# A block-product scheme for the up-projection of a channel mixer, with GpSimd forming the weight sums

## The chip, the cores and the metric

One NeuronCore of one Trainium2 chip runs the whole program. The metric is device time in microseconds of one execution; the time before is the median of three runs.

## What is computed

The program is one inference step of a one-layer decoder trunk on 520 tokens: 512 of a new prompt and 8 single-token samples. A token mixer (windowed attention beside a gated delta rule) is followed by a channel mixer, which is where the change lies. Cut to that part:

```python
x = x + rmsnorm(mix, ln_mix_post)
h = rmsnorm(x, ln_ffn_pre)                                   # 520 tokens x 2048
up, ffn_new = causal_dwconv(h @ w_ffn_in, ffn_buf, ffn_conv_w)  # 2048 -> 11264, then width 3 over tokens
gate, val = jnp.split(up + ffn_conv_b, 2, axis=-1)           # 5632 each
f = (jax.nn.gelu(gate, approximate=True) * val) @ w_ffn_out  # 5632 -> 2048
x = x + rmsnorm(f, ln_ffn_post)
```

All inputs and outputs are float32.

## The kernel before, in words

Features lie on the 128 partitions and tokens run along the free axis. Every large product is taken in three passes on TensorE: weights and operands are each split into a rounded part (`hi`) and a rest (`lo`), and hi x hi, hi x lo and lo x hi are added up in PSUM. ScalarE rounds (a cast, L127 for weights), VectorE subtracts (`lo`, L128). The tokens are kept as two parts, A of 256 and B of 264 columns, in pools `xsA` and `xsB`, 16 buffers each.

The stages follow each other in code order; a scheduler of the language places instructions on the engines, guided by priorities (`HI()` raises one) and explicit `issue_after` edges. Each engine then works through its own list in order. Weight loads are issued by SyncE (`Q`), and most small transfers of the mixer by GpSimd (`B`, `G`).

Stage 1 projects the inputs and runs the token mixer. Stage 2 is the output projection, once per token part; `mid2` then adds the residual, forms the FFN's operand `H2` and writes x1 to HBM. Stage 3 is the FFN. The 88 feature tiles of the up-projection are 44 gate tiles f and 44 value tiles 44 + f. `u_tile` makes one of them: 16 blocks of 128 rows by 3 passes by 2 token parts are 96 TensorE instructions (L160, in `gemm`). VectorE then multiplies by the norm's row (L1114) into `U`, and `pair` runs the width-3 convolution (ScalarE L1122, VectorE L1124 twice per tile), GeLU, the gating product (VectorE, L1134) and the split of the result into `act`. Two small GpSimd copies per tile (L1140, L1141) keep the last rows. After four f (a part p; there are 11), `ffn_out(p - 1)` runs the down-projection of the part before: 16 output tiles of 24 instructions, each added into `yacc` by VectorE (L1188). So up- and down-projection alternate. `part_end` handles the 8 samples of a part (L1159 to L1171).

The order of weights is the list `units`: `next_unit` keeps two units ahead of use, each loaded as two halves of 512 KB into `raw`, and each half split as two tiles of 128x512. The shifted caches are copied HBM to HBM in 128 pieces, three after each f (`shift(3)`).

Of the kernel before, what the change touches and what calls it, by code (L numbers as in the profile page):

```python
# [20 lines left out]
TAGS = ("bankS", "bankT", "bankP", "bankX")  # L21
NCV = 5
NA, NB = 256, 264
# [16 lines left out]
def trunk(ctx, tc, I, O):  # L40
# [51 lines left out]
    def ffn_units(p):  # L92
        u = []
        for f in range(4 * p, 4 * p + 4):
            u += [I["w_ffn_in"][f], I["w_ffn_in"][44 + f]]
        return u
    units += ffn_units(0) + ffn_units(0)
    for p in range(1, NP):
        units += ffn_units(p)
        units += [I["w_ffn_out"][p - 1, g].rearrange("p a b c -> p (a b) c") for g in range(4)]  # L100
    for _ in range(1):
        units += [I["w_ffn_out"][NP - 1, g].rearrange("p a b c -> p (a b) c") for g in range(4)]
# [5 lines left out]
    def emit_half(u, hf):  # L108
        with HI():
            raw = wraw.tile([128, 8, 128], F32, name="raw")  # L110
            lastw[0] = Q.dma_start(raw, units[u][:, hf * 8:hf * 8 + 8, :])
            if u >= len(units) - 4:
                # the last part is used twice: kept whole where the FFN's operand lay
                for q in range(4):
                    b = hf * 8 + q * 2
                    t = xsA.tile([128, 2, NA], F32R, name="xa") if q % 2 else xsB.tile([128, 2, NB], F32R, name="xb")
                    r = raw[:, q * 2:q * 2 + 2, :].rearrange("p a b -> p (a b)")
                    S.copy(t[:, 0, 0:256], r)  # L118
                    V.tensor_sub(t[:, 1, 0:256], r, t[:, 0, 0:256].bitcast(F32))
                    for j in range(2):  # L120
                        wt[u, "b", b + j] = (t[:, 0, j * 128:j * 128 + 128], t[:, 1, j * 128:j * 128 + 128])
                return
            for q in range(2):
                hi = whi.tile([128, 4, 128], F32R, name="hi")
                lo = wlo.tile([128, 4, 128], F32R, name="lo")
                r = raw[:, q * 4:q * 4 + 4, :]
                S.copy(hi, r)  # L127
                V.tensor_sub(lo, r, hi.bitcast(F32))  # L128
                wt[u, hf * 2 + q] = (hi, lo)
# [22 lines left out]
    def gemm(blks, X, ks, parts="AB"):  # L152
        ps = gps.tile([128, 1024], F32, name="ps")
        n = len(ks)
        for i, k in enumerate(ks):
            wh, wl = wblk(*blks[i])
            for j, (w, b) in enumerate(((wh, 0), (wh, 1), (wl, 0))):
                for part in parts:
                    o, w_ = SEG[part]
                    PE.matmul(ps[:, 256 + o:256 + o + w_], w, X[k][part][:, b, :],  # L160
# [3 lines left out]
    def split(dsts, src, o, w, scale=None):  # L164
        """dsts: fp32r tile [128,2,w]; src fp32 AP [128,w]."""
# [81 lines left out]
    def bias_tables():  # L247
        rb = Pd.tile([32, H], F32, name="rb")
        B.dma_start(rb, I["rel_bias"])
        for dst, o, n in ((FD, 0, 640), (FS, 640, 400)):  # L250
# [4 lines left out]
            for a in range(0, n, 512):  # L255
# [3 lines left out]
                if n == 640:  # L259
                    # the scores of the prompt are kept with the opposite sign  # L260
# [65 lines left out]
    # gates: rows 0..7 beta, rows 32..39 the decay  # L326
# [5 lines left out]
    def gates(ps):  # L332
# [29 lines left out]
    def gate_cols():  # L362
# [4 lines left out]
        # the samples' decay and beta on all partitions  # L367
# [30 lines left out]
    def col_sums(c, o, keep):  # L398
        """squared norms of q (o = 0) or k (o = 4), tokens of a chunk on partitions."""
# [147 lines left out]
    def scan(c):  # L547
# [48 lines left out]
        # state  # L596
# [12 lines left out]
        # outputs  # L609
# [32 lines left out]
    def over_partitions(rows):  # L642
        """sums over the partitions, on all of them."""
# [4 lines left out]
    def sample_dn():  # L648
# [16 lines left out]
        # partitions (sample, value head, half of dk)  # L665
# [80 lines left out]
    def rows_of(src, last):  # L746
        """[128 d, (h, b)] -> DRAM [b][h][d]: the queries, or the last row of a shifted cache."""
# [39 lines left out]
        # maximum over the rows of a sample  # L787
# [22 lines left out]
    def sample_values():  # L810
# [22 lines left out]
        # the new key and value  # L833
# [10 lines left out]
        # 16 rows carry the new key  # L844
# [82 lines left out]
    for idx, m in enumerate(mt_order):  # L927
# [11 lines left out]
        elif m < 8:  # L939
            with HI():  # L940
                V.scalar_tensor_tensor(attm[:, m, :], ps[:, 256:776], -SC, R1, op0=OP.mult, op1=OP.mult)
            V.tensor_copy(qs[:, m, :], attm[:, m, 512:520])
        elif m < 24:
            h = m % 8
            t = Ppa.tile([128, T], F32, name="kT" if m < 16 else "vT", bufs=2)
            with HI():
                V.tensor_mul(t, ps[:, 256:776], R1)
# [68 lines left out]
    R2 = rrow.tile([128, T], F32, name="R")  # L1016
    H2 = [{} for _ in range(KT)]

    def mid(part, also):
        """mix -> x1 = x + norm(mix) and the FFN's operand."""  # L1020
# [6 lines left out]
        for m in range(KT):  # L1027
# [18 lines left out]
    def mid2(part, acc, mxs, wk):  # L1046
        o, w = SEG[part]
        sl = xsA if part == "A" else xsB
        nm = "xa" if part == "A" else "xb"
# [4 lines left out]
        for g in range(8):  # L1054
            xr = wk.tile([128, 2, NB], F32, name="x2", bufs=2)
            x = xr[:, :, :w]
            Q.dma_start(x, I["xT"][:, 2 * g:2 * g + 2, o:o + w])
            y = mxs[g]
            V.tensor_mul(y, y, rp[:, None, :w].to_broadcast([128, 2, w]))
            V.tensor_add(x, x, y)  # L1060
            for j in range(2):
                m = 2 * g + j
                H2[m][part] = sl.tile([128, 2, w], F32R, name=nm)
                split(H2[m][part], xr[:, j, :w], o, w, scale=col(C_LN3 + m))
            a3 = acc3[:, :, :w]
            if g == 0:
                S.activation(a3, x, AF.Square)
            else:
                sq = wk.tile([128, 2, NB], F32, name="sq", bufs=1)
                S.activation(sq[:, :, :w], x, AF.Square)  # L1070
                V.tensor_add(a3, a3, sq[:, :, :w])
            Q.dma_start(X1D[:, 2 * g:2 * g + 2, o:o + w], x)
            yield
        norm_row(R2[:, o:o + w], acc3[:, :, :w], w, wk)
# [6 lines left out]

    mix_split("A", mxA)
# [7 lines left out]
    b_ = mid("B", lambda m, ev: after(ev, ga, m % 2))  # L1090
    run_all(ga)
    Pmb.close()
    Pw2 = ExitStack()
    gb = mid2("B", *b_, enter(pool("wk2"), Pw2))
    next(gb)
# [4 lines left out]
    fu = enter(pool("fu", side="right"))  # L1100
    fwc = lambda j, f: col(C_FW + j * FT + f)
    act = {}

    def u_tile(f, parts, U, early=False):
        u = next_unit()
        ps = gemm([(u, k) for k in range(KT)], H2, range(KT), parts=parts)
        o = SEG[parts[0]][0]
        w = sum(SEG[p][1] for p in parts)
        with HI():
            u, p = U[:, 2 + o:2 + o + w], ps[:, 256 + o:256 + o + w]  # L1110
            if early:
                S.copy(u, p)
                p = u
            return V.tensor_mul(u, p, R2[:, o:o + w])  # L1114
# [269 lines left out]
```

## Time and profile before

| quantity | value |
|---|---|
| median of 3 runs | 2528.92 us (2526.8 to 2529.82) |
| profiled execution, its span | 2524.7 us |
| TensorE busy | 2445.2 us, 97% |
| VectorE busy | 1478.5 us, 59% |
| ScalarE busy | 983.2 us, 39% |
| GpSimd busy | 206.7 us, 8% |
| mean granted TensorE clock | 0.986 |
| HBM read, written | 432.4 MB, 168.0 MB |

The span runs from the first to the last instruction of the profiled execution; it lies 4.2 us under the median of the timed runs. In rows of the profile, a line names the code line, the engine, the operation, output and input tiles, their shapes, and `x` a count; a mean is in ns, all else in us. PE is TensorE, PEld its weight loads, DVE VectorE, ACT ScalarE, POOL GpSimd and SP SyncE. TensorE's rows overlap, so that the mean of one is longer than the distance between two.

### The profile page before, as it was taken

The page shows a single profiled execution, that of the slowest core. Times are in us where ns is not written, and L with a number is a line of the kernel's source. Part 1 is how long each engine was busy: PE and PEld are TensorE (multiplying, and loading weights), DVE is VectorE, ACT ScalarE, POOL GpSimd, SP SyncE. Part 2 cuts the span into 40 slices and gives each one's busy share as a digit, 9 for nine tenths or more (in the row PEclk, how much of TensorE's full clock was granted, in tenths as well). Part 3 has the DMA queues.
Part 4 walks back from the last instruction along what each step waited for, and adds up shares of the span by engine and source line. Part 5 has one row for each costly group of instructions (what it writes and reads, how often), then busy time and mean ns, then how long its engine had stood idle before and what let it go on. Part 6 is the DMA issues. An engine that isn't in the chain of part 4 may idle for free.

```text
span 2524.7 us, 49670 instructions
## 1 busy us (share of the span) xinstructions
PE 2445.2 (97%) x20080; PEld 2424.1 (96%) x20080; DVE 1478.5 (59%) x3246; ACT 983.2 (39%) x2096; POOL 206.7 (8%) x470
## 2 busy tenths in 40 slices
PE   8499999998999999999999999999999999999996
PEld 7499999997999999999999999999999999999996
DVE  7379755676896567855454544445454545444467
ACT  6153244683335556632232323232323323232344
POOL 1120211212110000100000000000000000000000
PEclk9799999999999999999999999999999999999998
DMA  5663532559984567965564736364555546463753
GB/s 184 148 226 126 186 114 87 164 187 242 247 218 132 187 197 228 328 228 194 184 203 143 244 134 217 128 242 145 208 179 190 197 155 231 138 226 115 264 170 103
DMA packets 119061, 469.46 MB, mean 186 GB/s; under 512 B 20032, under 2 KB 39408, under 8 KB 116784
## 3 DMA queue, kind: packets, MB, share of 16 engines
q1 hardware_dynamic: 93648, 393.60, 46.1%
q0 software_dynamic: 25184, 72.69, 10.5%
q8 instruction: 158, 2.59, 0.4%
q14 instruction: 71, 0.58, 0.1%
HBM read 432.40 MB, written 167.97 MB: 238 GB/s over the span
## 4 chain that ended last, share of the span: by engine, by line
PE 85%; DMA 5%; DVE 4%; ACT 3%; issue 2%; another core or an unknown queue 2%; POOL 0%; SPq 0%; DVEq 0%; POOLq 0%; ACTq 0%
PE ps L160 80%; DMA pc<-in_cache_k_dram 2%; ACT prod L697 1%; DVE dtmp L706 1%; DMA raw<-in_w_out_dram 1%; DMA X1D<-x 1%; DMA raw<-in_w_ffn_out_dram 1%; PE bankX L513 1%; PE bankP L513 1%; DVE lo L128 0%; DVE sjk L783 0%; PE bankT L513 0%; PE bankS L513 0%; DMA out_s_rec_dram<-pc 0%
## 5 line engine op out<-in xcount | busy, mean ns | idle before, releaser
L160 PE MATMUL ps<-xb,hi 128*128 128x264 f32 x4640 | 1191.2, 287 | 0.0
L160 PE MATMUL ps<-xa,hi 128*128 128x256 f32 x4640 | 1181.2, 283 | 9.1 <-ACT xa L170 8.6
L127 ACT CAST hi<-raw 128x512 fp32r<-128x512 f32 x868 | 533.5, 619 | 1194.0 <-PE ps L160 1120.3
L160 PEld LDWEIGHTS ps<-xa,hi 128*128 128x128 f32 x4640 | 861.4, 190 | 14.3 <-ACT xa L170 8.6
L160 PEld LDWEIGHTS ps<-xb,hi 128*128 128x128 f32 x4640 | 861.4, 189 | 5.0 <-issue 2.7
L128 DVE TENSOR_TENSOR lo<-raw,hi 128x512 fp32r<-128x512 f32 x868 | 594.3, 689 | 462.5 <-ACT hi L127 460.7
L160 PE MATMUL ps<-xb,lo 128*128 128x264 f32 x2320 | 666.3, 287 | 3.1 <-DVE lo L128 1.5
L160 PE MATMUL ps<-xa,lo 128*128 128x256 f32 x2320 | 656.8, 283 | 0.0
L160 PEld LDWEIGHTS ps<-xb,lo 128*128 128x128 f32 x2320 | 438.2, 189 | 6.2 <-DVE lo L128 3.6
L160 PEld LDWEIGHTS ps<-xa,lo 128*128 128x128 f32 x2320 | 439.1, 189 | 0.8 <-issue 0.5
L160 PE MATMUL ps<-actB,hi 128*128 128x264 f32 x1280 | 337.1, 284 | 0.0
L160 PE MATMUL ps<-actA,hi 128*128 128x256 f32 x1280 | 333.3, 281 | 0.6 <-DVE yacc L1188 0.6
L160 PEld LDWEIGHTS ps<-actA,hi 128*128 128x128 f32 x1280 | 241.1, 188 | 0.8 <-ACT xb L118 0.8
L160 PEld LDWEIGHTS ps<-actB,hi 128*128 128x128 f32 x1280 | 240.5, 188 | 0.0
L1188 DVE TENSOR_TENSOR yacc<-yacc,ps 128x520 f32<-128x520 f32 (+2 forms) x176 | 113.8, 646 | 182.0 <-PE ps L160 180.5
L160 PE MATMUL ps<-actB,lo 128*128 128x264 f32 x640 | 181.7, 284 | 0.0
L160 PE MATMUL ps<-actA,lo 128*128 128x256 f32 x640 | 180.2, 282 | 0.0
L1124 DVE SCALAR_TENSOR_TENSOR gt<-U,cols,gt 128x512 f32<-128x512 f32 x176 | 131.9, 750 | 23.0 <-ACT gt L1122 20.9
L1140 POOL COPY pu<-U 128x2 f32<-128x2 f32 x88 | 49.7, 565 | 1136.6 <-DVE U L1114 1136.4
L1114 DVE TENSOR_TENSOR U<-ps,R 128x520 f32<-128x520 f32 (+2 forms) x92 | 61.1, 664 | 137.8 <-PE ps L160 137.7
L160 PEld LDWEIGHTS ps<-actA,lo 128*128 128x128 f32 x640 | 121.4, 190 | 0.0
L160 PEld LDWEIGHTS ps<-actB,lo 128*128 128x128 f32 x640 | 120.4, 188 | 0.0
(517 smaller groups left out, 2156.9 us busy)
## 6 DMA issues: line engine op xcount, KB each, us to landing
raw<-in_w_ffn_in_dram SPq DMA_DIRECT2D x192, 512.0 KB, 4.0
raw<-in_w_in_dram SPq DMA_DIRECT2D x98, 512.0 KB, 4.8
raw<-in_w_ffn_out_dram SPq DMA_DIRECT2D x88, 512.0 KB, 4.2
raw<-in_w_out_dram SPq DMA_DIRECT2D x64, 512.0 KB, 4.0
pc<-in_cache_k_dram POOLq DMA_DIRECT2D x24, 512.0 KB, 8.7
pc<-in_cache_v_dram POOLq DMA_DIRECT2D x24, 512.0 KB, 8.5
pc<-in_state_rec_dram POOLq DMA_DIRECT2D x16, 512.0 KB, 4.9
out_s_win_k_dram<-in_cache_k_dram SPq DMA_DIRECT2D x8, 1020.0 KB, 9.9
```

The source lines that it names most:

```text
L127: S.copy(hi, r)
L128: V.tensor_sub(lo, r, hi.bitcast(F32))
L160: PE.matmul(ps[:, 256 + o:256 + o + w_], w, X[k][part][:, b, :], start=(i == 0 and j == 0), stop=(i == n - 1 and j == 2))
L513: PE.matmul(p[:, j * 128:j * 128 + 128], lhs(4 * g + j), rhs(4 * g + j), start=True, stop=True)
L697: S.activation(dst[:, k], src(k), AF.Identity, scale=kqd[:, j, pc * 8 + k:pc * 8 + k + 1])
L706: V.tensor_reduce(dst, pr.rearrange("p k v -> p v k"), axis=AX.X, op=OP.add)
L1114: return V.tensor_mul(u, p, R2[:, o:o + w])
L1124: V.scalar_tensor_tensor(dst, U[:, j:j + 512], fwc(j, f), dst, op0=OP.mult, op1=OP.add)
L1140: G.tensor_copy(pu[:, s, i, :], U[:, 512:514])
L1188: ev = V.tensor_add(yacc[:, m, o:o + w], yacc[:, m, o:o + w], ps[:, 256 + o:256 + o + w])
```

## The change

The up-projection of a pair (f, 44 + f) is taken as a product of a 2 x 2 block matrix of weights (two halves of the 2048 inputs by the gate and the value tile) with a 2 x 2 block operand (the input halves by the token parts, now 260 columns each). The scheme is Winograd's form of Strassen's product: seven block products for eight. Weight blocks are B11 = X, B12 = W, B22 = Y, B21 = Z; each block is 128x1024. Operands are A11, A12, A22 and the sums S1 to S4, made once by `mid2`, which now also applies the norm's row ahead of the product.

What moves, by engine:

- TensorE: `product` issues 24 instructions (8 blocks, 3 passes) on one 260-column operand; an f has seven of them, A11, S4, S1, S2, S3, A12, A22.
- GpSimd: `wadd` sums weight blocks in place, four times an f (L1153): X + W, X + Y, Y + W, X + Z. It also takes one subtraction of results (L1328) and the gating product (L1252), which was on VectorE.
- ScalarE and VectorE: `hl` splits a block as one 128x1024 tile (L1140, L1141), seven times an f, since three of them are sums; the four split steps of the gated result leave this stage. VectorE adds up the seven results from PSUM (L1327 to L1341).
- Weight jobs run three ahead of their use (`JLOOK`), in four `hl` buffers. Raw buffers are `rx`, `ry` (two each), `rz`, `rw` (one each).
- For the first 16 f (`EARLY`) the products with A11 and A12 are taken in a stage of their own while `mid2` makes the B half's operands; their results go to HBM (`PD`) and come back, and those weight blocks are loaded again later.
- Gated results go to HBM (`ACT`), and the down-projection runs after all 44 f, in sweeps of two parts (the last part alone, by token halves), reading them back (`load_act`).

```diff
-NA, NB = 256, 264
+NA, NB = 260, 260
+EARLY = 16
...
+    def hl(raw):
+        t = whl.tile([128, 2, 8, 128], F32R, name="hl")
+        S.copy(t[:, 0], raw)
+        V.tensor_sub(t[:, 1], raw, t[:, 0].bitcast(F32))
+        return t
...
+    def wadd(t, other):
+        G.tensor_add(t, t, other)
...
+    def pre(f):
+        if f >= NFP or f in PRE:
+            return
+        PRE[f] = [wload(t, wblock(f, *b)) for t, b in
+                  (("rx", (0, 0)), ("rw", (0, 1)), ("ry", (1, 1)), ("rz", (1, 0)))]
+
+    def pair_jobs(f):
+        def b11():
+            pre(f)
+            X, W, Y, Z = PRE[f]
+            t = hl(X)
+            wadd(X, W)
+            return t
+
+        def b22():
+            pre(f)
+            X, W, Y, Z = PRE[f]
+            t = hl(Y)
+            if f < EARLY:
+                wadd(X, W)
+            return t
+
+        def t1():
+            X, W, Y, Z = PRE[f]
+            t = hl(X)
+            wadd(X, Y)
+            wadd(Y, W)
+            return t
+
+        def t2():
+            pre(f + 1)
+            X, W, Y, Z = PRE[f]
+            t = hl(X)
+            wadd(X, Z)
+            return t
+
+        def last(i):
+            return lambda: hl(PRE[f][i])
+
+        if f < EARLY:
+            jobs.extend([b22, t1, t2, last(2), last(0)])
+        else:
+            jobs.extend([b11, b22, t1, t2, last(2), last(3), last(0)])
...
+    def product(p, X, first=True):
+        w = next_w()
+        n = 0
+        for a, b in ((0, (0, 1)), (1, (0,))):
+            for k in range(8):
+                for c in b:
+                    PE.matmul(p[:, 0:NA], w[:, a, k, :], X[k][:, c, :], start=first and n == 0, stop=n == 23,
+                              skip_group_check=not first)
+                    n += 1
...
-        V.tensor_mul(gt, gt, vt)
-        t = act[f]
-        split(t["A"], gt[:, 0:256], 0, 256)
-        S.copy(t["B"][:, 0, 0:256], gt[:, 256:512])
-        V.tensor_sub(t["B"][:, 1, 0:256], gt[:, 256:512], t["B"][:, 0, 0:256].bitcast(F32))
+        G.tensor_mul(gt, gt, vt)
+        Q.dma_start(ACT[f], gt)
...
+        pe = bank("bankX")
+        product(pe, XC["S4"])
+        v = small("v")
+        with HI():
+            S.copy(v, pe[:, :NA])
+        pd = fbank("bd")
+        product(pd, XC["S1"])
+        pb = fbank("bb")
+        product(pb, XC["S2"])
+        u2, u3 = small("u2", 1), small("u3", 1)
+        with HI():
+            V.tensor_add(u2, u, pb[:, :NA])
+            G.tensor_sub(v, v, u2)
+        pc = fbank("bc")
+        product(pc, XC["S3"])
+        with HI():
+            V.tensor_add(u3, u2, pc[:, :NA])
+            V.tensor_sub(vb_, pd[:, :NA], u3)
+            V.tensor_add(va_, v, pd[:, :NA])
...
+    sweeps = [(2 * i, 2 * i + 1) for i in range(5)] + [(10,)]
```

Two places in the engines' orders, both from the middle of the up-projection. On GpSimd, before, each feature tile has two copies and one clearing of a new `U`:

```order
L1118 MEMSET U 128x2
L1140 COPY pu<-U 128x2
L1141 COPY su<-U 128x8
L1118 MEMSET U 128x2
L1140 COPY pu<-U 128x2
L1141 COPY su<-U 128x8
```

After, one f on GpSimd; `rx`, `ry`, `rz` and `rw` are the raw weight blocks X, Y, Z and W, `gt` the gate, `v` a result:

```order
L1153 TENSOR_TENSOR ry<-ry,rw 128x1024
L1304 MEMSET U 128x2
L1252 TENSOR_TENSOR gt<-gt 128x512
L1304 MEMSET U 128x2
L1153 TENSOR_TENSOR rx<-rx,rz 128x1024
L1328 TENSOR_TENSOR v<-v,u_20619 128x260
L1153 TENSOR_TENSOR rx<-rx,rw 128x1024
L1255 COPY pu<-U 128x2
L1256 COPY su<-U 128x8
L1153 TENSOR_TENSOR rx<-rx,ry 128x1024
```

The sums now stand between the small copies, and the next f's first sum (`rx` with `rw`) follows directly on this f's `v`. On VectorE, before, about one f:

```order
L1114 TENSOR_TENSOR U<-ps,R 128x520
L128 TENSOR_TENSOR lo<-raw,hi 128x512
L1124 SCALAR_TENSOR_TENSOR gt<-U,cols,gt 128x512 x2
L128 TENSOR_TENSOR lo<-raw,hi 128x512
L1134 TENSOR_TENSOR gt<-gt 128x512
L168 TENSOR_TENSOR actA<-gt,actA 128x256
L1138 TENSOR_TENSOR actB<-gt,actB 128x256
L128 TENSOR_TENSOR lo<-raw,hi 128x512 x2
```

After, one f on VectorE; `bb`, `bc`, `bd` are PSUM banks with results, `hl` the split weights:

```order
L1327 TENSOR_TENSOR u_22088<-u,bb 128x260
L1141 TENSOR_TENSOR hl<-rx,hl 128x1024
L1332 TENSOR_TENSOR u_22089<-u_22088,bc 128x260
L1333 TENSOR_TENSOR U<-bd,u_22089 128x260
L1334 TENSOR_TENSOR U<-v,bd 128x260
L1141 TENSOR_TENSOR hl<-ry,hl 128x1024
L1141 TENSOR_TENSOR hl<-rx,hl 128x1024
L1341 TENSOR_TENSOR U<-u_22088,bc 128x260
L1242 SCALAR_TENSOR_TENSOR gt<-U,cols,gt 128x512 x4
L1141 TENSOR_TENSOR hl<-rx,hl 128x1024
L1141 TENSOR_TENSOR hl<-ry,hl 128x1024
L1141 TENSOR_TENSOR hl<-rz,hl 128x1024
```

L1334 reads GpSimd's `v`, and the next weight splits stand behind it; each split of `rx` needs the GpSimd sum before it.

More of the change, by code (lines that the diff above doesn't have):

```diff
@@ L20 @@
 NB4 = 11
-TAGS = ("bankS", "bankT", "bankP", "bankX")
+TAGS = ["bankS", "bankT", "bankP", "bankX"]
 NCV = 5
-NA, NB = 256, 264
+NA, NB = 260, 260
+PO = 512 - NA
+EARLY = 16
 KT = 16
@@ L1073, in mid2, with scale @@
+            Q.dma_start(X1D[:, 2 * g:2 * g + 2, o:o + w], y)
             yield
-        norm_row(R2[:, o:o + w], acc3[:, :, :w], w, wk)
+        r2 = wk.tile([128, NB], F32, name="r2", bufs=1)
+        norm_row(r2, acc3, w, wk)
+        yield
+        def scale(g):
+            h = wk.tile([128, 2, NB], F32, name="x2", bufs=2 if part == "A" else 3)
+            for j in range(2):
+                V.scalar_tensor_tensor(h[:, j], mxs[g][:, j], col(C_LN3 + 2 * g + j), r2, op0=OP.mult, op1=OP.mult)
+            return h
@@ new lines, in mid2, with put @@
+        if part == "A":
+            for g in range(8):
+                h = scale(g)
+                for j in range(2):
+                    t = xsA.tile([128, 2, w], F32R, name="xa")
+                    split(t, h[:, j], 0, w)
+                    XC["A11" if g < 4 else "A12"][2 * (g % 4) + j] = t
+                yield
+            return
+        def put(name, i, src, pl):
+            for j in range(2):
+                t = pl.tile([128, 2, w], F32R, name="xb" if pl is xsB else "xs")
+                split(t, src[:, j], 0, w)
+                XC[name][2 * i + j] = t
@@ new lines, in whole @@
+        def whole(name, i):
+            a = wk.tile([128, 2, w], F32, name="ah", bufs=2)
+            for j in range(2):
+                t = XC[name][2 * i + j].bitcast(F32)
+                V.tensor_add(a[:, j], t[:, 0], t[:, 1])
+            return a
+        for i in range(4):
+            h1, h2 = scale(i), scale(4 + i)
+            put("A22", i, h2, xsB)
+            s = wk.tile([128, 2, w], F32, name="sd", bufs=2)
+            V.tensor_sub(s, h1, h2)
+            yield
+            a1, a2 = whole("A11", i), whole("A12", i)
+            V.tensor_sub(h1, a1, h1)
+            put("S3", i, h1, sxp)
+            put("S1", i, s, xsB)
+            yield
+            V.tensor_sub(s, s, a1)
+            put("S2", i, s, sxp)
+            V.tensor_add(a2, a2, s)
+            put("S4", i, a2, sxp)
+            yield
@@ L1089, in trunk @@
     next(ga)
-    b_ = mid("B", lambda m, ev: after(ev, ga, m % 2))
+    b_ = mid("B", lambda m, ev: after(ev, ga, 1))
     run_all(ga)
     Pmb.close()
-    Pw2 = ExitStack()
-    gb = mid2("B", *b_, enter(pool("wk2"), Pw2))
-    next(gb)
+    W1.close()
+    Gs.close()
     Pmx.close()
     P1s.close()
-    fu = enter(pool("fu", side="right"))
-    fwc = lambda j, f: col(C_FW + j * FT + f)
[L1102 to L1114, printed above, removed]
@@ new lines, in trunk, with raw_tile @@
+    TAGS[:] = ["bankS", "bankT", "bankP"]
+    NFP = 44
+    fwc = lambda j, f: col(C_FW + j * FT + f)
+    ACT = [dram.tile([128, 512], F32, name=f"ACT{f}") for f in range(NFP)]
+    PD = [dram.tile([128, 2, NA], F32, name=f"PD{f}") for f in range(EARLY)]
+    jobs = []
+    jst = dict(emitted=0, used=0)
+    def hl(raw):
[3 more added lines that the diff above has]
+        return t
+    def raw_tile(tag):
+        return wrx.tile([128, 8, 128], F32, name=tag, bufs=2 if tag in ("rx", "ry") else 1)
@@ L1147, in part_begin @@
         Q.dma_start(sst, I["state_ffn"][p])
-        for f in range(4 * p, 4 * p + 4):
-            act[f] = {q: fw.tile([128, 2, SEG[q][1]], F32R, name="act" + q, bufs=8) for q in "AB"}
         return pu, su, sst
@@ new lines, in trunk, with load_act @@
+    Fps.close()
+    Fs.close()
+    gp2 = enter(tc.tile_pool(name="gp2", bufs=2, space=bass.MemoryType.PSUM))
+    yac = enter(pool("yac", side="right"))
+    yacc = yac.tile([128, KT, T], F32, name="yacc")
+    fo = enter(pool("fo", side="right"))
+    act = {}
+    def load_act(f):
+        r = fo.tile([128, T], F32, name="ar", bufs=3)
+        Q.dma_start(r[:, 0:512], ACT[f])
+        G.tensor_copy(r[:, 512:520], sact[:, f])
+        act[f] = {}
+        for part, pl, n in (("A", xsA, "xa"), ("B", xsB, "xb")):
+            o, w = SEG[part]
+            act[f][part] = t = pl.tile([128, 2, w], F32R, name=n)
+            split(t, r[:, o:o + w], 0, w)
@@ L1177, in ffn_out @@
+    sweeps = [(2 * i, 2 * i + 1) for i in range(5)] + [(10,)]
+    runs = [(s, "AB") for s in sweeps[:-1]] + [(sweeps[-1], "A"), (sweeps[-1], "B")]
+    for s, parts in runs:
+        for g in range(4):
+            for hf in range(2):
+                for p in s:
+                    down_job(p, g, hf)
+    def ffn_out(s, parts, post=None):
         o = SEG[parts[0]][0]
@@ L1220, in trunk @@
+    for f in range(8):
+        load_act(f)
+    for i, s in enumerate(sweeps[:-1]):
+        for q in sweeps[i + 1]:
+            for f in range(4 * q, 4 * q + 4):
+                load_act(f)
+        ffn_out(s, "AB")
+        shift(8)
     shift(len(copies))
```

272 lines of the change are left out of this document (157 added, 115 removed).

## The prediction

> **What bounds the kernel now.** I read the page first: engine shares, then the chain that ended last.
>
> ```profile
> PE 2445.2 (97%) x20080; PEld 2424.1 (96%) x20080; DVE 1478.5 (59%) x3246; ACT 983.2 (39%) x2096; POOL 206.7 (8%) x470
> ...
> PE ps L160 80%; DMA pc<-in_cache_k_dram 2%; ACT prod L697 1%; DVE dtmp L706 1%; DMA raw<-in_w_out_dram 1%; DMA X1D<-x 1%; DMA raw<-in_w_ffn_out_dram 1%; PE bankX L513 1%; PE bankP L513 1%; DVE lo L128 0%; DVE sjk L783 0%; PE bankT L513 0%; PE bankS L513 0%; DMA out_s_rec_dram<-pc 0%
> ```
>
> The products at L160 are 80% of the chain. The second view is busy time by stretches; these two are one part of the FFN each, early and late (four feature tiles f, their up-projections and one part's down-projection):
>
> ```profile
> 1168.20:1306.30 138.10, 138.10 (x1155) 138.10 (x1154) 66.71 (x117) 42.02 (x74) 6.69 (x27) 1.00 0.54 186
> 2272.60:2410.50 137.90, 137.90 (x1153) 137.90 (x1153) 66.63 (x117) 41.83 (x74) 5.76 (x18) 1.00 0.58 194
> ```
>
> The columns are the stretch, its length, then PE, PEld, DVE, ACT, POOL busy, clock, DMA share, GB/s. PE never idles, at clock 1.00; DVE is busy 48%, ACT 30%, POOL 5%. By the code a part is 4 x 192 + 384 = 1152 products, so one costs 138.1 / 1152 = 0.120 us (0.1197 with the unrounded window mean). An f costs 192 x 0.1197 = 23.0 us, all 44 cost 1011 us. The third view is who waits for whom, over 1200 to 2300 us:
>
> ```profile
> ACT hi L127 <- PE ps L160: 691.8, 351, 2.5
> DVE lo L128 <- ACT hi L127: 258.0, 182, 2.2
> ```
>
> Weight preparation (ACT rounds, DVE subtracts) waits for PE to free buffers, not the other way. TensorE alone is the bound.
>
> **What the change removes from TensorE.** Seven products of 24 instructions replace 192: 168 per f, 7392 for 8448. The mean width stays 260. Gain: 1056 x 0.1197 = 126 us, 20.1 us an f, if everything else stays hidden. The 4224 products of the down-projection stay, in another order. This gain is real only if the weights arrive at one block of 128x1024 every 24 x 0.1197 = 2.87 us.
>
> **What it adds, by engine, per f.** Rows for the prices:
>
> ```profile
> L128 DVE TENSOR_TENSOR lo<-raw,hi 128x512 fp32r<-128x512 f32 x868 | 594.3, 689 | 462.5 <-ACT hi L127 460.7 <-PE ps L160 0.4
> L1124 DVE SCALAR_TENSOR_TENSOR gt<-U,cols,gt 128x512 f32<-128x512 f32 x176 | 131.9, 750 | 23.0 <-ACT gt L1122 20.9
> L473 DVE TENSOR_TENSOR b<-b,b 128x1024 f32<-128x1024 f32 x4 | 4.9, 1220 | 2.6 <-DMA b<-BRD 2.6
> L1042 DVE TENSOR_TENSOR acc<-acc,sqm 128x264 f32<-128x264 f32 x15 | 6.4, 428 | 0.0
> ...
> 1294.90 0.19 DVE L1162 TENSOR_TENSOR sy<-su,cols 128x32 f32<-128x32 f32 x1 [0.21 <-POOL su L1141]
> ...
> L127 ACT CAST hi<-raw 128x512 fp32r<-128x512 f32 x868 | 533.5, 619 | 1194.0 <-PE ps L160 1120.3 <-issue 24.6 <-DMA raw<-in_w_in_dram 22.0
> ```
>
> DVE: 7 subtractions of 128x1024 at 1.22 = 8.5; four convolution steps at 0.75 = 3.0; five steps on 260 columns of PSUM at 0.43 = 2.1; the samples' part 0.5 (eleven at 0.19, per four f). That is 14.2 of 20.1 us: as an engine it fits. ACT: the casts grow from 8 x 0.62 to 7 x 1.24, 3.7 us more on 42.0 / 4 = 10.5: it fits.
>
> SP: four loads of 512 KB an f as before, a store of the gated tile, cache copies. The load of rz waits for the last reader of the previous rz; behind it stand copies and the next rx, which is needed one f later, against this landing time:
>
> ```profile
> raw<-in_w_ffn_in_dram SPq DMA_DIRECT2D x192, 512.0 KB, 4.0
> ```
>
> So I cost the queue at nothing; its cover is those 20 us. The added traffic (32 early blocks read twice, gated tiles out and back) meets a DMA share of 0.54 to 0.58.
>
> GpSimd: four sums of 128x1024, one subtraction on 260 columns, the gating product on 512, and the small copies as before. No large GpSimd sum is in the trace, so it must be bounded. Two things matter: its price and whom it disturbs. Timeline, DVE then POOL, at the end of an f:
>
> ```profile
> 1086.41 0.70 DVE L1114 TENSOR_TENSOR U<-ps,R 128x520 f32<-128x520 f32 x1 [1.72 <-PE ps L160]
> 1087.02 0.68 DVE L128 TENSOR_TENSOR lo<-raw,hi 128x512 fp32r<-128x512 f32 x1
> ...
> 1087.17 0.58 POOL L1140 COPY pu<-U 128x2 f32<-128x2 f32 x1 [7.30 <-DVE U L1114]
> 1087.69 0.19 POOL L1141 COPY su<-U 128x8 f32<-128x8 f32 x1
> 1087.82 0.24 POOL L1154 COPY su<-sst 128x64 f32<-128x64 f32 x1
> ...
> L1140 POOL COPY pu<-U x88: 180/577/710, 1044.6 to 2409.9; 128x2 f32<-128x2 f32 x88
> ```
>
> A copy of two columns takes 0.58 us, one of eight 0.19: the first began under `lo`, a DVE step with two SBUF inputs (1087.02 to 1087.70), and ended 0.05 after it. Over all 88 its minimum, median and maximum are 180, 577 and 710 ns. The opposite direction:
>
> ```profile
> 295.71 0.54 POOL L321 COPY b<-b 128x256 f32<-128x256 f32 x1 [9.78 <-DMA b<-in_state_dn_conv_dram]
> ...
> 295.68 1.05 DVE L312 TENSOR_TENSOR b<-b,cwh 128x128 f32<-128x128 f32 x3 [0.48 <-DMA b<-in_state_dn_conv_dram]
> ...
> L312 DVE TENSOR_TENSOR b<-b,cwh x3: 336/416/514, 295.7 to 296.3; 128x128 f32<-128x128 f32 x3
> ```
>
> Three equal DVE steps beside two POOL copies take 336, 416 and 514 ns. I read this as one engine at a time at SBUF: DVE steps with two SBUF operands and GpSimd steps that read SBUF exclude each other. The Trainium skill says so outright ("SBUF — State Buffer", Who interferes with whom): of those two kinds, the second to issue fully blocks until the first is done. This trace agrees with its 577 against 180 ns.
>
> Price of a sum: if the shortest DVE step is the first, it ended at 295.68 + 0.34 = 296.02, and the copy of 256 columns ended at 296.25: 0.23 us, 0.9 ns a column. The 64- and 8-column copies give the same slope, (237 - 186) / 56 = 0.91. One operand at that rate is 0.17 + 0.93 = 1.1 us: the low end. Read, read and write one after the other, three passes, is 3.0: the high end. Two operands through one interface are 0.17 + 1.86 = 2.0, which I take: a sum differs from the copy by one operand read. Subtraction 0.64, gating product 1.1, copies 2 x (0.18 + 0.19) + 0.24 / 4 = 0.8.
>
> **The sum.** Exclusive time in an f: DVE 8.5 + 3.0 + 0.5 = 12.0 (PSUM steps excluded), POOL 4 x 2.0 + 0.64 + 1.1 + 0.8 = 10.5. Together 22.6 us, over the 20.1 of TensorE. I use whole durations, so the 0.08 by which rows overlap stands for the hand-overs. The orders let it be almost gapless, as the next f's sums stand among this f's evictions. What waits: DVE's L1334 waits for GpSimd's `v`, behind it the next weight subtractions, behind those TensorE. For the first 16 f two subtractions fewer: 20.1, against only 14.4 of TensorE; they hide nothing more, and their two other products ran earlier.
>
> - 28 f at 22.6 = 633; 16 f at 20.1 = 322; 32 early products at 2.87 = 92: 1047 against 1011, +36.
> - Early stage: DVE does 32 x 1.22 = 39 for weights and the B half's operands: 24 wide steps at 0.70 to the r row, 16 scalings at 0.49, 40 splits at 0.42, 16 wide at 0.70, 16 joins at 0.43, 60 together. 99 against 92: +7.
> - Two stage changes (weight buffers refill before it, gated tiles come back after it): 0 to 12, a 4.0 load with a 1.2 cast and a 1.2 subtraction at each end; I take 5. The end reads the last part twice but drops its 32 small splits: 0.
>
> ```profile
> L1071 DVE TENSOR_TENSOR acc<-acc,sq 128x528 f32<-128x528 f32 x7 | 4.9, 705 | 0.0
> L171 DVE SCALAR_TENSOR_TENSOR xa<-x,cols,xa 128x256 fp32r<-128x256 f32 x16 | 7.1, 482 | 0.0
> L168 DVE TENSOR_TENSOR actA<-gt,actA 128x256 fp32r<-128x256 f32 x44 | 18.6, 424 | 14.2 <-ACT actA L167 14.2
> ```
>
> Total +48 on the profiled span of 2524.7; the median of the runs, 2528.9, lies 4 above it. Forecast: 2577 us. A measurement tells about 0.2%, 5 us, from no change.
>
> A page has its own price: the Trainium skill ("GPSIMD Engine Reference", section 3.1) gives 4497 ns for a GpSimd add of 2048 fp32; half, 2.25 us, is an estimate from that page, which no run here shows, and would make the sum 44 us more, 2621.
>
> **Rivals.**
> - *TensorE stays the bound; the two engines share SBUF well enough.* For it: GpSimd does not hold SBUF through its whole instruction when it computes long:
>
> ```profile
> 447.40 10.95 POOL L657 TENSOR_TENSOR dr<-dr,mhalf 128x64 f32<-128x64 f32 x1 [1.49 <-DVE dr L656]
> ...
> 450.29 0.69 DVE L128 TENSOR_TENSOR lo<-raw,hi 128x512 fp32r<-128x512 f32 x1 [2.39 <-ACT hi L127]
> ```
>
> `lo` took its usual 0.69 inside. Against it: 64 columns may be read ahead, 1024 hardly. It decides from a held time per sum of about 1.7 us: 176 sums x 0.27 = 48. At 1.1 us an f is 20.1 and 16.5: 563 + 264 + 92 = 919, -92 + 12, about 2449. With no exclusion at all, -126 + 12: 2415.
> - *GpSimd starves.* DVE's stream without gaps can keep it out for several steps:
>
> ```profile
> 982.93 2.24 POOL L184 TENSOR_TENSOR nr_s<-nr_s,mhalf 88x3 f32<-88x3 f32 x1 [98.12 <-DVE nr_s L183]
> 983.17 0.68 DVE L128 TENSOR_TENSOR lo<-raw,hi 128x512 fp32r<-128x512 f32 x1
> 983.77 0.68 DVE L1071 TENSOR_TENSOR acc<-acc,sq 128x512 f32<-128x512 f32 x1
> ...
> L184 POOL TENSOR_TENSOR nr_s<-nr_s,mhalf x8: 701/785/2236, 41.3 to 2506.8; 128x2 f32<-128x2 f32 x4, 88x3 f32<-88x3 f32 x4
> ```
>
> Three columns for 2.24 us, where 0.70 is the minimum of that line: it waited out `lo` and `acc`. If each sum then comes one subtraction late (1.22) and nothing else fits in between for half of them, 44 x 4 x 0.61 = 107 more: 2684. Against it: after two sums DVE itself needs their result.
> - *No measurable change:* sums near 1.7 us, 2524 to 2534.
>
> **Chances.** Port-bound, 2534 to 2650 (sums from 1.75 to 2.4 us): 0.55. Starved, or a sum near its high end (3.0: 176 more, 2753), above 2650: 0.08. Unmeasurable: 0.07. Sharing better, 2435 to 2524: 0.20. TensorE-bound near 2415: 0.10. Slower 0.63, same 0.07, faster 0.30. The range 2435 to 2650 leaves out the last and the starved case, 0.18; the likeliest one's own range is 2534 to 2650.
>
> **What would show it.** GpSimd's L1153 rows at 2.0 us or longer by what they wait; DVE's L1141 above 1.22; TensorE idle in the up-projection, released by DVE `hl`; an f period near 22.6 late and 20.1 early; the down-projection unchanged, 384 products in 46 us. Wrong if PE stays at 99% there with a period of 20.1: then the exclusion costs nothing.
>
> The orders behind this are in the section on the change.

## The result and the profile after

The changed kernel takes 2603.08 us in the median of four runs (2600.95 to 2605.05), against 2529.37 for the kernel before beside them: ratio 1.029, interval 1.0275 to 1.0304. The profiled execution took 2601.33 us with a span of 2599.3, 74.6 more than the span before. The page of the kernel after, shares of the span and the 40 slices of three engines:

```profile
PE 2370.8 (91%) x19078; PEld 2330.5 (90%) x19078; DVE 1875.6 (72%) x3130; ACT 1082.8 (42%) x2032; POOL 879.0 (34%) x778
...
PE   8499999997999998987777999999999799999996
DVE  7379654666986577988878899999999734434338
POOL 1120211111100000287777777877777400000000
```

TensorE has 1002 records fewer. It idles most in slices 19 to 22 (the first 16 f) and in slice 32 (the turn to the down-projection); the stretch in which VectorE and GpSimd are both dense is slices 18 to 31. The windows, columns as in the prediction, are the early products, the first 16 f, the last 28 f, the turn to the down-projection, and most of that:

```profile
983.40:1087.00 103.60, 98.68 (x806) 98.27 (x807) 91.60 (x153) 60.88 (x113) 5.77 (x4) 0.97 0.80 259
1087.00:1419.50 332.50, 260.99 (x1951) 250.46 (x1950) 270.73 (x271) 120.22 (x148) 252.94 (x196) 0.95 0.79 267
1419.50:2048.10 628.60, 578.07 (x4672) 569.75 (x4670) 591.78 (x542) 285.14 (x373) 475.57 (x339) 0.99 0.72 249
2048.10:2058.30 10.20, 0.00 (x0) 0.00 (x0) 4.29 (x9) 3.08 (x7) 1.96 (x6) 0.68 0.75 242
2058.30:2530.00 471.70, 468.35 (x3875) 467.31 (x3876) 185.37 (x251) 113.89 (x169) 9.98 (x41) 1.00 0.37 117
```

A late f takes 628.6 / 28 = 22.45 us at clock 0.99, an early one 332.5 / 16 = 20.8. TensorE is busy 92% of the late stage, VectorE 94%, GpSimd 76%. But much of VectorE's 94% is not work. These are groups of VectorE in the late stage and of GpSimd in the whole run:

```profile
L1141 DVE TENSOR_TENSOR hl<-rx,hl 128x1024 fp32r<-128x1024 f32 x112 | 151.3, 1353 | 7.0 <-ACT hl L1140 5.6
L1242 DVE SCALAR_TENSOR_TENSOR gt<-U,cols,gt 128x512 f32<-128x512 f32 x112 | 134.7, 1255 | 24.6 <-ACT gt L1240 24.6
L1141 DVE TENSOR_TENSOR hl<-ry,hl 128x1024 fp32r<-128x1024 f32 x56 | 134.5, 2401 | 0.2
L1141 DVE TENSOR_TENSOR hl<-rz,hl 128x1024 fp32r<-128x1024 f32 x29 | 83.1, 2867 | 0.0
L1275 DVE TENSOR_TENSOR sy<-su,cols 128x32 f32<-128x32 f32 x14 | 15.9, 1133 | 1.5 <-POOL su L1256 1.5
L1333 DVE TENSOR_TENSOR U<-bd,u 128x260 f32<-128x260 f32 x28 | 12.0, 429 | 1.0
...
L1153 POOL TENSOR_TENSOR rx<-rx,rz 128x1024 f32<-128x1024 f32 x44 | 138.4, 3146 | 8.5 <-DVE hl L1141 8.5
L1153 POOL TENSOR_TENSOR rx<-rx,ry 128x1024 f32<-128x1024 f32 x44 | 110.8, 2519 | 50.7 <-DVE hl L1141 50.7
```

One form of subtraction, one size: 1.35 us on `rx`, 2.40 on `ry` and 2.87 on `rz`, where 1.22 was the price before. (The three counts make 197 for 28 f, seven an f; the order of VectorE shown ahead ends before the last `rx` of its f. Of the four splits of `rx` in an f, the first takes the loaded block and needs no sum.) The convolution step went from 0.75 to 1.26, the samples' 32 columns from 0.19 to 1.13. Steps that take an operand from PSUM stayed at 0.43. Side by side, in one late f, VectorE and then GpSimd:

```profile
1701.31 2.35 DVE L1277 TENSOR_TENSOR sy<-sy,cols 128x32 f32<-128x32 f32 x1
...
1719.65 3.42 DVE L1141 TENSOR_TENSOR hl<-rx,hl 128x1024 fp32r<-128x1024 f32 x1
...
1701.23 2.38 POOL L1153 TENSOR_TENSOR rx<-rx,rz 128x1024 f32<-128x1024 f32 x1
...
1718.39 0.77 POOL L1267 COPY su<-sst 128x64 f32<-128x64 f32 x1
1719.12 2.87 POOL L1153 TENSOR_TENSOR ry<-ry,rw 128x1024 f32<-128x1024 f32 x1
```

A step of 32 columns began 0.08 us after a GpSimd sum and ended (1703.66) 0.05 after the sum's end (1703.61): it took 2.35 us for 0.19 of work. The subtraction at 1719.65 outlasted the sum that ended at 1721.99 by 1.08, about its own work. Nothing in a row marks such a wait; it counts as busy. Who waits for this, from 1200 to 2000 us:

```profile
ACT hl L1140 <- POOL rx L1153: 237.5, 90, 5.8
...
PEld bb L1232 <- ACT hl L1140: 36.5, 12, 4.4
PE bb L1232 <- ACT hl L1140: 33.9, 11, 4.2
PE bc L1232 <- DVE u L1332: 29.1, 26, 1.7
```

ScalarE waits for the sums before it can round them, and TensorE for ScalarE and VectorE. In the kernel before, those waits ran the other way. VectorE itself hardly waits for ScalarE's rounding in the late stage (5.6 us on `rx`, nearly nothing on `ry` and `rz`, in the rows above): for 94% of the time it is at work or held up inside its rows.

The 74.6 us: the up-projection from its first to its last product took 1064.0 us against 1011 (+53), the turn without TensorE 10.9 (2047.4 to 2058.3), the FFN's first product came 5.9 later (983.42, before 977.56), and 4.8 are left for the down-projection and the end.

### The profile page after: what moved, and what is told of

Same layout as the page of the kernel before. It is cut to its first block, busy times and chain, and to the rows that moved or that the text cites. A ratio compares the mean times of both kernels' runs of the same rounds, so it can differ in the third digit from the quotient of the medians.

```text
span 2599.3 us, 47873 instructions
## 1 busy us (share of the span) xinstructions
PE 2370.8 (91%) x19078; PEld 2330.5 (90%) x19078; DVE 1875.6 (72%) x3130; ACT 1082.8 (42%) x2032; POOL 879.0 (34%) x778
## 5 line engine op out<-in xcount | busy, mean ns | idle before, releaser
L1410 PE MATMUL ps<-xa,hl 128*128 128x260 f32 x2112 | 486.7, 283 | 14.6 <-ACT xa L147 13.3
L1410 PE MATMUL ps<-xb,hl 128*128 128x260 f32 x2112 | 486.3, 284 | 4.0 <-DVE yacc L1417 4.0
L140 PE MATMUL ps<-xa,hi 128*128 128x260 f32 x1824 | 471.8, 290 | 9.1 <-ACT xa L150 8.4
L140 PE MATMUL ps<-xb,hi 128*128 128x260 f32 x1824 | 472.1, 290 | 0.0
L1410 PEld LDWEIGHTS ps<-xa,hl 128*128 128x128 f32 x2112 | 386.0, 189 | 16.4 <-ACT xa L147 14.0
L1410 PEld LDWEIGHTS ps<-xb,hl 128*128 128x128 f32 x2112 | 384.7, 188 | 4.7 <-issue 2.6
L140 PEld LDWEIGHTS ps<-xa,hi 128*128 128x128 f32 x1824 | 339.6, 191 | 13.3 <-ACT xa L150 8.4
L1140 ACT CAST hl<-rx 128x1024 fp32r<-128x1024 f32 x203 | 210.2, 1049 | 335.8 <-POOL rx L1153 280.7
L140 PEld LDWEIGHTS ps<-xb,hi 128*128 128x128 f32 x1824 | 339.3, 191 | 4.4 <-issue 2.4
L1141 DVE TENSOR_TENSOR hl<-rx,hl 128x1024 fp32r<-128x1024 f32 x203 | 290.6, 1433 | 42.1 <-ACT hl L1140 40.4
L109 ACT CAST hi<-raw 128x512 fp32r<-128x512 f32 x324 | 197.5, 618 | 289.9 <-PE ps L140 245.8
L110 DVE TENSOR_TENSOR lo<-raw,hi 128x512 fp32r<-128x512 f32 x324 | 220.5, 687 | 123.6 <-ACT hi L109 122.4
L1141 DVE TENSOR_TENSOR hl<-ry,hl 128x1024 fp32r<-128x1024 f32 x131 | 246.6, 1882 | 45.2 <-ACT hl L1140 44.5
L1140 ACT CAST hl<-ry 128x1024 fp32r<-128x1024 f32 x131 | 137.4, 1049 | 170.5 <-PE ps L1410 94.1
```

Source lines behind the costliest of these rows:

```text
L140: PE.matmul(ps[:, PO + o:PO + o + w_], w, X[k][part][:, b, :], start=(i == 0 and j == 0), stop=(i == n - 1 and j == 2))
L1140: S.copy(t[:, 0], raw)
L1141: V.tensor_sub(t[:, 1], raw, t[:, 0].bitcast(F32))
L1410: PE.matmul(ps[:, PO + o_:PO + o_ + w_], t[:, a, i * 4 + k, :], act[4 * p + k][part][:, b, :], start=n == 0, stop=n == last)
```

## Experiments

The theory: VectorE steps with two SBUF operands and GpSimd steps that read SBUF exclude each other for a whole instruction, and the sum of their times is the period. Rivals: the late sums stand in a chain and delay the weights whoever makes them; GpSimd's and SP's queues; a price of sharing that is less than a whole instruction.

### One operation moved, one taken out

The sums on VectorE, all else as in the changed kernel:

```diff
     def wadd(t, other):
-        G.tensor_add(t, t, other)
+        V.tensor_add(t, t, other)
```

> All four weight sums of an f go to VectorE, nothing else changes. Theory (two-operand VectorE steps and SBUF-reading GpSimd steps exclude each other, and their sum of times set the period of 22.4 us late and 20.8 early): the exclusive time falls to 12.0 + 4 x 1.22 + 2.8 left on GpSimd = 19.7 us, VectorE's own to 19.1, both under TensorE's 20.1, so a late f takes 20.1 to 20.8 and an early one, where 17.3 stand against 14.4 of TensorE, 17.3 to 18.5. The run falls by 28 x 1.9 + 16 x 2.9 = 100, to about 2500 us (2480 to 2530). Rival 1 (VectorE as an engine is what is full: it was busy 592 of 629 us late): 4.9 us more work on it makes it slower, 2700 or more. Rival 2 (the length of the chain split, sum, split sets the period, not sharing): a sum shrinks from 2.35 to 1.22 in the chain, but waits its turn on VectorE; 2540 to 2600.

Measured: 2475.14 us (2474.1 to 2477.14), ratio to the kernel before 0.9784 (0.9767 to 0.98). Its late stage, then one group of splits and one of sums, both counted over the whole run:

```profile
1352.30:1918.10 565.80, 562.72 (x4682) 561.78 (x4681) 533.81 (x652) 287.59 (x373) 172.19 (x228) 1.00 0.80 281
...
L1141 DVE TENSOR_TENSOR hl<-ry,hl 128x1024 fp32r<-128x1024 f32 x131 | 161.1, 1230 | 43.9 <-ACT hl L1140 43.8
...
L1153 DVE TENSOR_TENSOR rx<-rx,rz 128x1024 f32<-128x1024 f32 x44 | 53.5, 1216 | 0.0
```

TensorE is busy 99.5% and an f takes 20.21 us. VectorE got 112 sums more in this stage (4 x 28) and its busy time *fell* from 592 to 534: a sum costs it 1.22 us and costs GpSimd 2.35 or more, and during a sum there VectorE's steps with two SBUF operands stood still. The run lies 5 us under its expected range, as an early f took 16.6 us where 17.3 to 18.5 was expected. That VectorE is full by its own work (rival 1) is out. The chain of rival 2 is still in place but its sums are shorter, so this run speaks against it only by the time, 65 us under what that rival expected.

The next kernel keeps most of GpSimd's time but not its reading: the sums are left out, and two clearings of the same block stand in the place of each, two operations of 0.95 us for one of 2.35.

```diff
     def wadd(t, other):
-        G.tensor_add(t, t, other)
+        G.memset(t, 0.5)
+        G.memset(t, 0.25)
```

> Each weight sum is replaced by two GpSimd clearings of the same tile, which read nothing from SBUF and take about 2.1 us against 2.35; the sums themselves are left out. Theory (exclusion through SBUF reads): the period drops to TensorE's 20.1 us late, and to 14.5 to 16 early, though GpSimd works as long: 2603 - 28 x 2.3 - 16 x 5.5 = about 2450 (2430 to 2490). Rival 2 (GpSimd's time in the chain, or its queue, sets the period): 0.25 us less a sum gives at most 44 x 1 = 44, so 2560 to 2600. Rival 1 (VectorE is full by its own work): no change, 2590 to 2605.

Measured: 2524.29 us (2515.81 to 2529.01), ratio 0.9969 (0.9951 to 0.9986): between the two expectations. The late stage speaks for the exclusion, the early one does not follow. Late window, then rows of the waits from 1107 to 1384 us, and rows of GpSimd's and ScalarE's timelines there:

```profile
1384.40:1960.70 576.30, 566.25 (x4688) 565.65 (x4687) 397.77 (x541) 283.75 (x373) 343.75 (x450) 0.99 0.74 256
...
ACT hl L1140 <- POOL rx L1154: 83.0, 28, 6.2
...
PE bb L1233 <- DVE u L1328: 12.9, 1, 12.9
...
DVE sy L1273 <- DMA sst<-in_state_ffn_dram: 9.5, 1, 9.5
...
1253.65 1.66 POOL L1329 TENSOR_TENSOR v<-v,u 128x260 f32<-128x260 f32 x1 [4.58 <-DVE u L1328]
1255.25 0.95 POOL L1153 MEMSET rx<- 128x1024 f32 x1
1256.26 0.95 POOL L1154 MEMSET rx<- 128x1024 f32 x1
...
1257.24 1.05 ACT L1140 CAST hl<-rx 128x1024 fp32r<-128x1024 f32 x1 [6.15 <-POOL rx L1154]
...
1265.08 3.03 POOL L1253 TENSOR_TENSOR gt<-gt 128x512 f32<-128x512 f32 x1 [0.17 <-ACT gt L1252]
```

Late: 20.58 us an f, TensorE 98.3%, VectorE's 592 us of busy time are 398, with as many instructions (541 for 542). The fall of the period alone does not decide: two clearings take about 1.9 us from start to start, a sum 2.30 (measured below), so GpSimd's own time fell by 1.6 us an f too, and the late f by 1.87. What decides is that VectorE's rows shrank by a third, and that VectorE was not waiting for the chain in the changed kernel.

Early: 17.25 us an f where 14.5 to 16 was expected, the mean of the last 15. The first early f took 46.0 us (1079.15 to 1125.18), against 20.0 in the changed kernel: a VectorE step waited 9.5 us for a transfer (`sst`), and TensorE 12.9 for the VectorE step behind it. So 26 of the 66 us between the expected 2450 and the profiled 2515.81 come from this one f, where the order of the loads differs: SP issued that transfer 25 us after the last early product, and 2.4 after it in the changed kernel. ScalarE still waits 83 us for GpSimd in the window. The clearings stand in GpSimd's queue behind `v`, which waited 4.58 us for VectorE before ScalarE's longest wait ended, and behind the gating product, which reads SBUF and took 3.03 us. So some of the early stage's time is that queue, not the sums' reading; how much was not separated.

### All of it on VectorE, or one sum on GpSimd

```diff
-        G.tensor_add(t, t, other)
+        V.tensor_add(t, t, other)
...
-        G.tensor_mul(gt, gt, vt)
+        V.tensor_mul(gt, gt, vt)
...
-            G.tensor_sub(v, v, u2)
+            V.tensor_sub(v, v, u2)
```

> The four sums, the subtraction of results and the gating product all go to VectorE; GpSimd keeps only small copies. Theory: exclusive time 18.0 + 0.8 = 18.8 us late, but VectorE's own time 14.2 + 4.9 + 0.4 + 0.7 = 20.2, as long as TensorE's 20.1, and 17.8 against 14.4 early: a late f 20.5 to 21.5, an early one 18 to 19, 10 to 40 us slower than with the sums alone on VectorE, about 2520 (2495 to 2560). Rival 2 (chain): no dependence on GpSimd is left, so it should be the fastest of all, below 2480.

Measured: 2470.2 us (2461.89 to 2471.85), ratio 0.9755 (0.9737 to 0.9773). The expected loss against the first experiment did not come. The time is what rival 2 had forecast (below 2480), so this run by itself does not speak for the exclusion against the chain. Windows of the last 15 early f and of the late stage:

```profile
1106.30:1353.20 246.90, 227.97 (x1827) 223.79 (x1826) 239.07 (x344) 114.37 (x141) 40.22 (x94) 0.98 0.96 347
1353.20:1919.10 565.90, 562.57 (x4661) 560.74 (x4659) 513.21 (x706) 288.18 (x371) 58.71 (x172) 1.00 0.80 277
```

Late, VectorE carries everything with 513 us, 18.3 an f. I had expected 20.2, by adding whole durations; rows on VectorE overlap by about 0.08 each. Early, VectorE is at 97% and the DMA share at 0.96, at 16.5 us an f (246.9 / 15); which of the two sets that period is open.

Between the ends, one sum of four stays on GpSimd (Y + W):

```diff
-    def wadd(t, other):
-        G.tensor_add(t, t, other)
+    def wadd(t, other, eng=V):
+        eng.tensor_add(t, t, other)
...
-            wadd(Y, W)
+            wadd(Y, W, G)
```

> Three sums on VectorE, Y + W alone stays on GpSimd. Theory: exclusive time 12.0 + 3.7 + 2.35 + 2.8 = 20.8 us late and 18.4 early, VectorE's own 17.9: a late f 20.8 to 21.3, an early one 18.4 to 19.4, so 15 to 40 us slower than with all four on VectorE: about 2525 (2500 to 2550). Rival (VectorE is full by its own work): 1.2 us an f less on it than with all four, 50 us faster than that run. Rival 2 (chain): Y + W is on no chain longer than X's, so no difference from all four on VectorE, within 5 us.

Measured: 2512.5 us (2507.01 to 2512.93), ratio 0.9924 (0.9909 to 0.9939); 18.73 us an early f, 20.47 a late one. As the theory has it for the early f, a little less late. Both rivals fail: rival 2 expected no difference, and the run is 37 us slower than the first experiment, from which it differs by this one sum, and 42 slower than all on VectorE. So one GpSimd sum an f, on no chain longer than X's, costs 37 us of the 128 that four cost (2475.14 to 2603.08, taken across two chips whose kernels before differ by 2).

### The lock by itself

The kernel before, with stretches of 128x1024 steps ahead of everything, engine against engine; the time of that run has no meaning.

```diff
+        for i in range(6):
+            G.tensor_add(mg[i % 2], ma, mb_)
...
+        for i in range(6):
+            G.tensor_add(mg[i % 2], ma, mb_)
+        for i in range(10):
+            V.tensor_sub(mv[i % 2], mc, md)
...
+        for i in range(18):
+            V.tensor_sub(mv[i % 2][:, 0:512], mp, md[:, 0:512])
...
+        for i in range(14):
+            G.memset(mg[i % 2], 1.0)
+        for i in range(10):
+            V.tensor_sub(mv[i % 2], mc, md)
```

> The kernel before, with five short stretches of test instructions ahead of its first stage (its time is of no interest): six GpSimd sums of 128x1024 alone; six VectorE subtractions of 128x1024 alone; six sums beside ten such subtractions; six sums beside eighteen VectorE subtractions of 512 columns with one operand in PSUM; fourteen GpSimd clearings beside ten two-operand subtractions. Theory (exclusion): alone 2.35 and 1.22 us; beside each other the six and ten take the sum of their times, 6 x 2.3 + 10 x 1.14 = 25 us, with rows of one engine lengthened by those of the other; with an operand in PSUM both run as if alone, 18 x 0.62 = 11 us beside 14; the clearings and the subtractions likewise, 14 us beside 11.4. Rival (the two share SBUF evenly, finely interleaved, and slow down by less than the sum): 14 to 20 us for the third stretch. Rival (no exclusion): 14 us, the longer of the two.

Minimum, median and maximum in ns, then first and last start. Sums alone (L92), subtractions alone (L95), the two together (L98, L100), sums with subtractions from PSUM (L104, L106), clearings with subtractions (L110, L112):

```profile
L92 POOL TENSOR_TENSOR mg<-ma,mb x6: 2327/2327/2358, 5.8 to 17.3; 128x1024 f32<-128x1024 f32 x6
L95 DVE TENSOR_TENSOR mv<-mc,md x6: 1214/1215/1225, 23.1 to 28.7; 128x1024 f32<-128x1024 f32 x6
L98 POOL TENSOR_TENSOR mg<-ma,mb x6: 3313/3315/3373, 31.2 to 47.7; 128x1024 f32<-128x1024 f32 x6
L100 DVE TENSOR_TENSOR mv<-mc,md x10: 1210/3354/3362, 29.9 to 53.1; 128x1024 f32<-128x1024 f32 x10
L104 POOL TENSOR_TENSOR mg<-ma,mb x6: 2348/2348/2352, 58.3 to 69.8; 128x1024 f32<-128x1024 f32 x6
L106 DVE TENSOR_TENSOR mv<-bankS,md x18: 673/673/676, 54.3 to 64.5; 128x512 f32<-128x512 f32 x18
L110 POOL MEMSET mg<- x14: 946/946/967, 72.1 to 84.3; 128x1024 f32 x14
L112 DVE TENSOR_TENSOR mv<-mc,md x10: 1215/1219/1226, 72.4 to 82.6; 128x1024 f32<-128x1024 f32 x10
```

A sum beside subtractions takes 3.31 and a subtraction beside sums 3.35: they take turns, one instruction each. From start to start a sum alone is (17.3 - 5.8) / 5 = 2.30 and a subtraction (28.7 - 23.1) / 5 = 1.12; a pair in turns is (47.7 - 31.2) / 5 = 3.30, no more than both in sequence (3.42). The stretch of six and ten took 24.5 us (29.88 to 54.34), as the exclusion has it (25); both rivals, 14 to 20 and 14, are out. So for these two forms the exclusion is complete and the hand-over costs nothing. Neither subtractions with a PSUM operand nor clearings change with what runs beside them. The Trainium skill ("SBUF — State Buffer", Who interferes with whom) has a lock held through the whole instruction, and only against a GpSimd operation that reads SBUF: both agree with these rows. The first does not agree with the GpSimd step of 64 columns and 10.95 us in the prediction, inside which a subtraction with two SBUF operands took its usual 0.69; the measurement decides, and how long such a step holds SBUF stays open.

### The turn to the down-projection

In the changed kernel, the last f's store and the first reloads on SP's queue, then the first cast and product:

```profile
2054.21 0.33 SPq L1253 DMA_DIRECT2D ACT<-gt  x1
2054.59 1.39 SPq L1358 DMA_DIRECT2D ar<-ACT  x3
...
2057.88 0.41 ACT L147 CAST xa<-ar 128x260 fp32r<-128x260 f32 x1 [5.19 <-DMA ar<-ACT]
...
2058.34 0.80 PE L1410 MATMUL ps<-xa,hl 128*128 128x260 f32 x2 [10.94 <-ACT xa L147]
```

The first reload belongs to a part stored long before, but stands behind the store of f = 43, which waits for that tile's gating. To take that away, the version with all on VectorE issues the last store from GpSimd's queue, and fills the samples' columns of `ar` on ScalarE:

```diff
-        Q.dma_start(ACT[f], gt)
+        (B if f == NFP - 1 else Q).dma_start(ACT[f], gt)
...
-        G.tensor_copy(r[:, 512:520], sact[:, f])
+        S.copy(r[:, 512:520], sact[:, f])
```

> The version with all sums and products of results on VectorE, and at the change from up- to down-projection two edits: the last gated tile is stored from GpSimd's queue, so that the reloads of the first gated tiles do not stand behind that store on SyncE, and ScalarE instead of GpSimd copies the samples' columns into reloaded tiles. Theory (the 10 us without TensorE there are the queue behind the last store): the gap falls to 4 to 6 us and the run by 4 to 7, to 2465. Rival (the reloads wait for buffers that only the last product frees): no change, within 2 us.

Measured: 2469.64 us (2464.26 to 2481.2), ratio 0.9772 (0.9751 to 0.9792), no different from the same version without the edit (below). The rival's "no change" is what the time shows. The gap fell from 9.8 us there to 7.8, about half of the least that was expected. SP's queue and the VectorE row that its first load waits for:

```profile
1917.46 1.23 DVE L1141 TENSOR_TENSOR hl<-ry,hl 128x1024 fp32r<-128x1024 f32 x1 [0.32 <-ACT hl L1140]
...
1918.71 0.34 SPq L1149 DMA_DIRECT2D ry<-in_w_ffn_out_dram  x1
1919.10 1.37 SPq L1358 DMA_DIRECT2D ar<-ACT  x3
```

The reloads now stood behind a weight load that waits for its buffer, `ry`, to be read. The next waiter in the queue took the place of the first. What the second edit, the copies on ScalarE, did was not measured by itself.

Two runs more, the early products for 18 f in place of 16 (on top of the last edit), and the version with all on VectorE once more, on the same chip:

```diff
-EARLY = 16
+EARLY = 18
```

> As the run before it, with 18 early f for 16. Theory: each f moved costs 5.7 us of TensorE in the early stage unless VectorE is still the longer there (99 against 92 with 16, 104 against 103 with 18), and 16.5 for 20.2 later: 2 x (3.7 - 2.4 to 5.7), so -3 to +4 us, no difference to be measured.

> All sums and result products on VectorE, once more beside the two runs before it, to compare on one chip: 0.976 of the kernel before, 2465 to 2475 us.

Measured: 2467.22 us (2463.58 to 2471.05), ratio 0.9757 (0.9743 to 0.9771), for 18 early f; 2469.34 (2464.2 to 2474.23), ratio 0.9763 (0.9747 to 0.9779), for all on VectorE. The three can't be told apart. The version with all on VectorE, without these edits, beats the kernel before by 2.4% and the changed one by 5%.

## Why the prediction was right, point by point

The sign and the mechanism were right: the port-bound case, given 0.55, is what happened, and the time lies in its range, 26 us above its value. The size of the change was not: +74.6 us of span where +48 was forecast. The terms:

- *TensorE's gain.* 20.1 us an f where all is hidden: 20.21 with the sums on VectorE. Right.
- *Price of a sum, 2.0 us.* Mis-sized: 2.33 to 2.35 unblocked. Two operands did not cost just one read more than a copy. The estimate from the Trainium skill ("GPSIMD Engine Reference", section 3.1), 2.25 by halving, came nearer and is still 0.08 low; the sum that used it, 2621, missed by 18 the other way.
- *A late f, 22.6.* Measured 22.45, but that it came so near is luck: two errors cancel. The sums are 1.4 us dearer an f; against that, the 0.08 by which rows overlap, which I set aside for the hand-overs, was not spent. Measured from start to start, VectorE has 7 x 1.12 + 4 x 0.66 + 0.3 = 10.8 and GpSimd 4 x 2.30 + 2.3 for the rest = 11.5: 22.3.
- *An early f, 20.1.* Measured 20.8, 10 us over 16 f. The same count from start to start gives 20.1 here, so 0.7 an f is something else; the experiment with clearings points to GpSimd's queue in this stage, but did not settle it.
- *Early stage, 99 for VectorE against 92 for TensorE.* Measured 103.6, but not for that reason: VectorE is busy 91.6 of them and TensorE 98.7, with 806 records for the 768 products, at clock 0.97. TensorE's one wait there of any size is 4.9 us for ScalarE's copies of results (L1291).
- *Two stage changes, 0 to 12, taken as 5.* Measured 10.9 at the turn and 5.9 at the FFN's start, of which 1.7 stood already at the end of the output projection (its last product at 979.16, before 977.44): 15.1, outside that range. In the other 4.2 at the start the first weight cast (982.33) stands on ScalarE behind four casts of `x`. At the turn I priced a load, a cast and a subtraction, and missed that the reload's place in SP's queue is behind a store that waits for the last f's gating.
- *The end, 0.* 4.8, found only as the remainder. Of the eleven blocks of 384 down-projection products, the nine in the middle take 46.1 to 46.2 us, as the prediction's sign had it (46), the first 52.1 and the last 53.7; the kernel before has losses of its own in its FFN (1526.0 us for 12672 products, 1516.8 at 0.1197).

The misses of the parts of the up-projection sum to +10.7, those of the two stage changes, with the 1.7, to +11.8, of the down-projection and end to +4.8. Less 0.7 us that both the late window and the turn count, that is the 26.6 between the forecast +48 and +74.6. So the largest miss is the stage changes; the price of a sum, too low by 0.33, hardly shows in the total because of the overlap that cancels it.

The rival that the two engines share well enough fell with the alternating rows (3.31 for 2.33); the price per sum at which it decided, 1.7 us of held time, was passed by far. GpSimd did not starve in the changed kernel: the sums' mean is 2.74, not 2.35 + 0.61 and more. That the sums' place in the chain sets the late period fell with the one sum left on GpSimd and with VectorE's rows in the run with clearings. Most signs came true: VectorE's L1141 rose, GpSimd's L1153 was above 2.0, TensorE waited in the up-projection, though released more often by ScalarE's round of a late sum than by VectorE's rest of it. The path that I named did not: VectorE's L1334 does not appear among the waits for GpSimd's `v`; from 1200 to 2000 us it is `v` that waits 81.8 us for VectorE's `u` (L1327).

## What to carry to other kernels

Before moving elementwise work from VectorE to GpSimd, add the times of both engines' steps that read SBUF (two operands on VectorE's side) as if one engine did them, from start to start; if the sum passes the bound, the move costs time even where GpSimd has idle time. Here each of the sums was cheaper on the engine that looked fuller (1.22 against 2.33 us). Ask of a busy share how much of it is longer rows: compare the mean of one form with its minimum before calling an engine full. And when a read-back follows a store on one in-order queue, look at what the store waits for.

## What the runs showed of the hardware

In the side-by-side run the alternation is strict, one instruction of each engine in turn, and free of hand-over cost: pairs of 2.30 and 1.12 us came every 3.30. GpSimd's clearing of 128x1024 floats (0.95 us), which reads nothing, does not take part in it. A VectorE step of 32 columns cost 2.35 us by it in the changed kernel, 0.19 by itself. And with an engine's own rows overlapping by 0.08, a sum of durations overstated VectorE by a tenth (20.2 against 18.3 an f), which was enough to make the version with all on VectorE look like a loss against the first experiment.
